# Twenty-three modulation vectors summed on VectorE instead of multiplied on TensorE

## The chip, the cores and the metric

The kernel runs on one core of one Trainium2 chip. The metric is the device time of one execution in microseconds (us), the median over several runs. Engines: PE is TensorE (PEld its weight load), DVE is VectorE, ACT is ScalarE, POOL is GpSimd, SP is SyncE. A name with q (SPq, POOLq) is an engine's own instruction queue, from which it also issues transfers.

## What is computed

Two blocks work on 256 tokens of width 1024. The first has two layers, each a gated feed-forward net, a mixer and a second gated net. Layer 0's mixer is a state-space scan (ssd) and also reads 256 context tokens, layer 1's is a pooling mixer. The second block has two layers of attention and an expert layer ("peer": 8 heads choose among 16384 experts). Every sub-layer takes a scale, a shift and a gate that depend on a conditioning vector `c`, not on the tokens:

```
m  = (silu(c)     @ ada_w[i] + ada_b[i]).reshape(-1, 9, 1024)      # first block, i = 0, 1
mc = (silu(c_ctx) @ ada_w[i] + ada_b[i]).reshape(9, 1024)          # the same for the context
x  = x + 0.5 * m[:, 2] * swiglu(modulate(x, g, m[:, 0], m[:, 1]), wg, wu, wd)
h  = h + 0.5 * mc[2] * swiglu(modulate(h, g, mc[0], mc[1]), wg, wu, wd)   # context, layer 0 only
mod = c_2_act @ w_ada + b_ada                                      # second block: 6 vectors a layer
```

That is 9 + 9 + 6 + 6 = 30 modulation vectors, each a product of one row of 1024 numbers with a 1024 x 1024 float32 matrix, 4 MB that is read once. The context needs a second result only for vectors 0 to 4 of layer 0, since nothing after the ssd mixer reads it.

## The kernel before

**Work on TensorE.** Activations stand as 8 tiles of 128 features by 256 tokens (512 with the context). Each weight unit, 128 x 1024 float32 (512 KB), is loaded by SP into one of four buffers (`raw`), and split in halves of 512 columns: ACT rounds a half to `whi` (L444), DVE subtracts to get `wlo` (L446). Three matmuls (`mm3`: low x high, high x low, high x high) then give float32 precision. `pump` keeps the splits three halves ahead of TensorE (`LS` = 3). The order in time: the first feed-forward net f0 (512 columns), the ssd mixer, f1 (256), f2, the pooling mixer, f3, attention 0, expert layer 0, attention 1, expert layer 1. Within a net, `ffn_up` takes 22 blocks of two units each (gate and up; psum tile `gu`), and after a block DVE and ACT make the product (`ft`, `sg`, `gh`, `gl`); `ffn_down` takes 8 blocks of three units (`dn`).

**The modulation vectors.** A vector is eight steps, one for each 128 rows of its matrix. A step (`ada_mm`) is four matmuls at four groups of 32 columns of the array: 32 columns of `sc` (silu of the conditioning vectors, three of them used) against 256 columns of the row tile each, summed in psum over the eight steps. In the profile it is eight PE instructions on the tile `ada`. After the eighth, ACT copies the result (`adarow`, L568), TensorE transposes it twice (`adat`, L575) and DVE adds the bias (`mods`, L581). Two vectors are made at the start (`adah`, `adar`), since nothing can begin without them.

**Where the other 28 stand.** In f0, f1 and f2 the planner `mix` puts row tiles among the weight units as units of their own, two at a time, and four at the end of a net (`KEEP`), where TensorE waits for a norm. SP loads them in that order, through the same queue. In the ssd mixer and the attentions the order on every engine is made by `Flow`, a list scheduler with a cost for each operation. There `ada_load` and `ada_work` are chains beside the others: 52 steps go into the ssd stage and 44 into the two attentions, in groups of two (ssd) or one (attention).

**Other names.** `btab` is a table of attention biases, written by POOL to DRAM in f0 (L1633); `csts` holds constants, `xt` the inputs; `rel` and `bk` feed the bias table. `Gen.need` makes sure that a vector is ready before its first reader.

Of the kernel before, what the change touches and what calls it, by code (L numbers as in the profile page):

```python
# [31 lines left out]
ATT_ADA = (3, 3)  # L32
# [11 lines left out]
SSD_ADA = 7  # L44
# [182 lines left out]

class Flow:
# [4 lines left out]
    TABLE_US, DMA_US, ADA_US, FAST, SOON, MORE = 1.28, 1.46, 3.5, 0, 2, 1  # L233

    def __init__(self, gen, slots, ada, raws, lat, early=0, group=1):
        slots = {**slots, "W": [f"W{n}" for n in range(gen.LS + 1)], **{k: [x for x in raws if x[0] == k] for k in "QR"}}
# [12 lines left out]
        self.adas, self.raws = {}, raws  # L249
        self.spawn(self.ada_load(ada, early), 0)  # L250
        self.spawn(self.ada_work(ada, group), 9)
# [108 lines left out]
    def ada_load(self, keys, early):  # L360
        for n, key in enumerate(keys):
            r = self.adas[key] = yield "take", "Q" if n < early else "R"
            yield "S", self.ADA_US if n >= self.FAST else self.DMA_US
            self.gen.nc.sync.dma_start(self.raws[r], self.gen.ada_src(*key))
            self.loading(("ada",) + key)

    def ada_work(self, keys, group):
        g = self.gen
        for n in range(0, len(keys), group):
            part = keys[n:n + group]  # L370
            yield "wait", *[("ada",) + k for k in part]
            yield "P", 0.43 * len(part)
            for key in part:
                g.ada_mm(key[3], self.raws[self.adas[key]])
                self.give(self.adas[key])
                self.set(("used",) + key)
            if key[3] == KT - 1:
                yield "A", 0.26
                self.spawn(self.ada_fin(key[:3], g.ada_row()), 1)

    def ada_fin(self, key, row):
        t = yield "take", "T"
        self.gen.ada_tag = t
        g = self.gen.ada_fin(*key, row)
        yield "P", 0.23
        next(g)
        yield "V", 0.1
        next(g, None)
        self.give(t)
        self.set(("mod",) + key)  # L390


class Gen:
    def __init__(self, tc, I, out):
        self.tc, self.nc, self.I, self.out = tc, tc.nc, I, out
        self.units = []
        self.subs = []
        self.cur = self.nd = self.ns = self.csub = 0
        self.raw, self.hl = {}, {}
        self.later = deque()  # L400
        self.sides = []
        self.ln_loaded = False
        self.ada_tag, self.no_split = "B", True
        self.loaded = set()
        self.ada_pool, self.took = None, {"w": deque(maxlen=self.LD), "ada": deque(maxlen=self.LA)}
        self.uid = 0
        self.sq_bufs = 2
# [3 lines left out]
    SSD_GROUP, ATT_GROUP, SSD_LAT, ATT_LAT = 2, 1, 0.06, 0.04  # L411
    LD, LD2, LA, LS, SUB, NW, SSD_Q = 4, 8, 4, 3, 512, 12, 8

    def add(self, tag, ap, n, kind="w"):
        u = len(self.units)
        self.units.append((tag, ap, n, kind))
        if kind == "w":
            for c in range(0, n, self.SUB):
                self.subs.append((u, c, min(self.SUB, n - c)))

    def room(self, i):

        if self.ada_pool is None:
            return i < self.cur + self.LD
        k = self.units[i][3]
        last = self.took[k]
        return len(last) < last.maxlen or last[0] not in self.raw

    def pump(self):
        while self.nd < min(len(self.units), self.cur + self.LD + self.LA) and self.room(self.nd):  # L430
            self.load(self.nd, self.p_raw)
# [20 lines left out]
    def load(self, i, pool):  # L452
        if self.units[i][0][0] == "gu" and len(self.units[i][0]) == 6 and self.units[i][0][5] == 0:
            t = self.p_first.tile([128, 512], F32, tag="first", name=f"raw{i}", bufs=2 * self.FIRST)
        else:
            kind = self.units[i][3] if self.ada_pool is not None else "w"
            if kind == "ada":
                t = self.ada_pool.tile([128, 1024], F32, tag="araw", name=f"raw{i}", bufs=self.LA)
            else:
                t = pool.tile([128, 1024], F32, tag="raw", name=f"raw{i}")  # L460
            self.took[kind].append(i)
# [5 lines left out]
    def _next(self):  # L467
        i = self.cur
        self.cur += 1
        self.pump()  # L470
        self.run_later()
        return i
# [20 lines left out]
    def get(self, tag, width=128):  # L493

        while self.units[self.cur][3] == "ada":
            self.ada_step()
# [35 lines left out]
    def ada_unit(self, which, l, m, k):  # L532
        self.add((which, l, m, k), self.ada_src(which, l, m, k), 1024, "ada")

# [3 lines left out]

    def ada(self, n):
        for _ in range(n):  # L540
            if self.cur < len(self.units) and self.units[self.cur][3] == "ada":
                self.ada_step()

    def ada_step(self):
        nc = self.nc
        i = self.cur
        self.cur += 1
        which, l, m, k = self.units[i][0]
        self.ada_mm(k, self.raw.pop(i))
        if k == KT - 1:  # L550
            row = self.ada_row()
            self.mod_sent.add((which, l, m))
            self.defer(4, lambda: [None for _ in self.ada_fin(which, l, m, row)])
        self.pump()
        self.run_later()
# [9 lines left out]
    def ada_row(self):  # L565
        self.uid += 1
        row = self.p_ada.tile([128, 256], F32, tag="adarow", name=f"adarow{self.uid}")
        self.nc.scalar.copy(row, self.ada_ps)  # L568
        return row

    def ada_fin(self, which, l, m, row):
# [5 lines left out]
        ns = 2 if which == 0 and l == 0 else 1  # L577
# [7 lines left out]
    def need(self, *keys):  # L585
        if not all(k in self.mod_ready for k in keys):
            left = {k for k in keys if k not in self.mod_ready and k not in self.mod_sent}
            while left and self.units[self.cur][3] == "ada":
                self.ada_step()
                left -= self.mod_sent  # L590
# [94 lines left out]
    def open_fed(self):  # L685
# [9 lines left out]
        self.ada_pool = self.p_ada  # L695
# [93 lines left out]
    def ffn_up(self, l, j, N, gh, gl, x, post, pw, first=0):  # L789

        for f in range(first, FT):
            ps = []
# [11 lines left out]
    def ffn_down(self, l, j, N, gh, gl, xs, gate_m, fed):  # L804
# [7 lines left out]
        self.ln_table()  # L812
        for d in range(KT):
            p = self.ps.tile([128, 512], F32, tag="C", name=f"dn{l}{j}{d}")
# [5 lines left out]
            for s, x in enumerate(xs):  # L820
                nc.vector.scalar_tensor_tensor(x[:, d], p[:, 256 * s:256 * s + 256], hg[s][:, d:d + 1],
                                               x[:, d], op0=ALU.mult, op1=ALU.add)
            if fed:
# [5 lines left out]
    FIRST = 3  # L829

    def ffn0(self, xs):
# [6 lines left out]
        with ExitStack() as es:  # L838
            es.enter_context(self.sqpool("f00"))
            pu = es.enter_context(self.pool("ffu"))  # L840
# [126 lines left out]
            gh = pg.tile([128, FT, N], F32R, name="gh")  # L967
            gl = pg.tile([128, FT, N], F32R, name="gl")
            self.ada_pool = pg
            bt = self.bias_table(pw)  # L970
# [13 lines left out]
            self.ffn_up(0, 0, N, gh, gl, lambda k: (uh[:, k], ul[:, k]), lambda: post, pw, self.FIRST)  # L984
            self.ffn_down(0, 0, N, gh, gl, xs, 2, None)
            self.ada_pool = None
# [39 lines left out]
    def ssd(self, XL, XC, px, u, fed):  # L1026
# [9 lines left out]
        with ExitStack() as es:  # L1036
# [10 lines left out]

            raws = {f"Q{n}": T1(f"sraw{n}", [128, 1024]) for n in range(2)}
            for n, (k, s) in enumerate((("m0", [4, 128]), ("m1", [4, 128]), ("hin", [4, 2, 64]), ("yo", [4, 2, 64]))):
                x = raws[f"Q{n // 2}"][:, n % 2 * 512:n % 2 * 512 + 512]  # L1050
                B[k] = x.rearrange("p (a b) -> p a b", a=4) if n < 2 else x.rearrange("p (a b c) -> p a b c", a=4, b=2)
                slots[k] = [k]
            raws.update({f"R{n}": XC[:, 4 * n:4 * n + 4].rearrange("p a b -> p (a b)") for n in range(2)})
            fl = Flow(self, {**slots, **{k: self.banks[k] for k in "ABCT"}}, self.ssd_ada, raws, self.SSD_LAT, self.SSD_Q,
                      self.SSD_GROUP)
# [31 lines left out]
            def rs_work():  # L1087
# [8 lines left out]
                for n in range(2):  # L1096
                    yield "wait", *[("u", k, x) for k in range(4 * n, 4 * n + 4) for x in range(2)]
                    fl.give(f"R{n}")
                fl.give("gr.0")
                fl.give("sq.0")  # L1100

            def early_work():
                yield "wait", *[("used",) + k for k in self.ssd_ada[self.SSD_Q - 2:self.SSD_Q]]
                for k in ("m0", "m1", "hin", "yo"):
                    fl.give(k)
# [409 lines left out]
            for k in ("T", "gr", "R", "m0", "m1", "hin", "yo"):  # L1515
                fl.free[k] = []
            fl.spawn(early_work(), 0)
# [101 lines left out]
    def bias_table(self, pool):  # L1619
# [11 lines left out]
        sb = pool.tile([8, 384], F32, name="bts")  # L1631
# [4 lines left out]
    def attention(self, l, XL, fed):  # L1636
# [5 lines left out]
        with ExitStack() as es:  # L1642
            es.enter_context(self.sqpool(f"at{l}"))
            self.p_ada = es.enter_context(self.pool(f"adap2{l}", 2))
            p2 = es.enter_context(self.pool(f"rawp2{l}"))
# [4 lines left out]
            for j in range(4):  # L1650
                for kv in range(2):
# [30 lines left out]
            raws = {f"R{n}": p2.tile([128, 1024], F32, name=f"R{n}_{l}") for n in range(self.LD2)}  # L1682
            st = {}
            fl = Flow(self, {"A": self.banks["A"] + self.banks["C"], "B": self.banks["B"], "T": self.banks["T"],
                             "w": list(work), "v": list(wide)}, self.att_ada[l], raws, self.ATT_LAT, group=self.ATT_GROUP)
# [435 lines left out]
    def peer(self, l, XL, last, fed, px):  # L2121
# [5 lines left out]
        with ExitStack() as es:  # L2127
# [57 lines left out]
            for e in range(120):  # L2185
                if e + 1 == 64:
                    self.side_rest()
                    er.close()
                    tail = es.enter_context(self.pool(f"pet{l}")).tile([128, 2, 4, 256], F32R, name=f"tail{l}")
                if e + 1 < 120:  # L2190
# [5 lines left out]
                wq.pop(e)  # L2196
            self.p_sq = Slices(act[0])
# [301 lines left out]
    GROUP, KEEP, QUIET, EVERY, HOLD = 2, 4, 5, 2, 4  # L2499

    def mix(self, gen, ada=(), every=1, start=0, bounds=()):


        a = deque(x for w in ada for x in ([w] if len(w) == 4 else [w + (k,) for k in range(KT)]))
        gen = list(gen)
# [121 lines left out]
```

## Time and profile before

| | us |
|---|---|
| median of 3 runs (lowest, highest) | 3321.62 (3319.46, 3324.21) |
| the profiled execution's own time | 3323.24 |
| span of its instructions | 3321.5 |
| PE busy | 3286.7 (99%) |
| DVE busy | 2356.7 (71%) |
| ACT busy | 1690.9 (51%) |
| POOL busy | 21.6 (1%) |

The page gives busy time by engine for the one profiled execution. PE's busy time overstates its work, since matmuls are pipelined and their ends are modelled; what a group of matmuls costs is read from the starts of what stands before and behind it. The mean granted clock of TensorE is 0.998 of full speed. 622 MB are moved, 187 GB/s on the mean.

### The profile page before, as it was taken

To read this page: it belongs to the slowest core of one execution; us is meant where nothing else is said; L and a number is where in the kernel's file an instruction comes from. 1 tells how busy PE (TensorE), PEld (TensorE's weight loads), DVE (VectorE), ACT (ScalarE), POOL (GpSimd) and SP (SyncE) were. 2 spreads that over 40 slices of the span, in tenths; PEclk is the share of its full clock that TensorE was granted. 3 is DMA by queue.
4 is the path that set the end of the run, shared out by engine and by line. 5 is a ranking of instruction groups with operands and counts; after the bars stand their busy time and mean duration, and the time that the engine had idled before them with its cause. 6 is when DMAs were issued, how large, how long until landed. Compare 5 with 4: busy or idle time off the path is not lost.

```text
span 3321.5 us, 71394 instructions
## 1 busy us (share of the span) xinstructions
PE 3286.7 (99%) x28517; PEld 3063.8 (92%) x28532; DVE 2356.7 (71%) x5253; ACT 1690.9 (51%) x3408; POOL 21.6 (1%) x40
## 2 busy tenths in 40 slices
PE   7999999999999999999999999999999999999999
PEld 5777778889999989989999999999889999999999
DVE  4333378886656667677898779866778888788765
ACT  4222255555555555566554444455666554444454
POOL 0000000000000000000000000000000000000000
PEclk9999999999999999999999999999999999999999
DMA  7644444446777655675555444455665554444554
GB/s 249 182 178 173 176 150 162 143 156 227 253 240 249 231 195 187 183 271 185 177 184 168 165 164 162 161 178 185 227 230 169 179 185 161 164 163 162 172 185 159
DMA packets 177790, 621.97 MB, mean 187 GB/s; under 512 B 19949, under 2 KB 23021, under 8 KB 177072
## 3 DMA queue, kind: packets, MB, share of 16 engines
q1 hardware_dynamic: 174912, 609.07, 54.2%
q0 software_dynamic: 2544, 8.32, 1.0%
q8 instruction: 224, 3.67, 0.5%
q14 instruction: 110, 0.90, 0.1%
HBM read 614.69 MB, written 2.62 MB: 186 GB/s over the span
## 4 chain that ended last, share of the span: by engine, by line
PE 97%; DMA 1%; DVE 1%; ACT 1%; issue 0%; SPq 0%; ACTq 0%; DVEq 0%
PE s L522 22%; PE up L522 22%; PE gu L522 18%; PE dn L522 9%; PE xbc L522 4%; PE ada L522 3%; PE g L522 3%; PE q L522 3%; PE wc L522 3%; PE wo L522 3%; PE z L522 1%; PE yd L522 1%; PE st L522 1%; DMA raw<-ffn_gu 1%; PE sc L522 0%; PE yo L522 0%
## 5 line engine op out<-in xcount | busy, mean ns | idle before, releaser
L446 DVE TENSOR_TENSOR wlo<-raw,whi 128x512 fp32r<-128x512 f32 x1846 | 1254.2, 685 | 732.0 <-ACT whi L444 713.4
L444 ACT CAST whi<-raw 128x512 fp32r<-128x512 f32 x1846 | 1126.3, 615 | 1009.9 <-PE up L522 376.1
L522 PE MATMUL s<-U,whi 128*128 128x256 f32 x4096 | 734.0, 281 | 0.0
L522 PE MATMUL up<-U,whi 128*128 128x256 f32 x3936 | 705.1, 282 | 0.0
L522 PEld LDWEIGHTS s<-U,whi 128*128 128x128 f32 x4096 | 632.4, 189 | 0.0
L522 PEld LDWEIGHTS up<-U,whi 128*128 128x128 f32 x3936 | 606.2, 189 | 0.0
L522 PE MATMUL s<-U,wlo 128*128 128x256 f32 x2048 | 581.3, 284 | 0.0
L522 PE MATMUL up<-U,wlo 128*128 128x256 f32 x1968 | 556.2, 283 | 0.0
L522 PEld LDWEIGHTS s<-U,wlo 128*128 128x128 f32 x2048 | 386.9, 189 | 0.0
L522 PEld LDWEIGHTS up<-U,wlo 128*128 128x128 f32 x1968 | 371.9, 189 | 0.0
L522 PE MATMUL gu<-U,whi 128*128 128x258 f32 x1408 | 254.4, 282 | 2.5 <-DVE U L732 2.5
L522 PEld LDWEIGHTS gu<-U,whi 128*128 128x128 f32 x1408 | 218.7, 190 | 3.3 <-DVE U L732 3.1
L522 PE MATMUL dn<-gh,wlo 128*128 128x256 f32 (+1 forms) x704 | 220.2, 313 | 0.3 <-DVE wlo L446 0.3
L522 PE MATMUL dn<-gl,whi 128*128 128x256 f32 (+1 forms) x704 | 218.2, 310 | 0.0
L522 PE MATMUL dn<-gh,whi 128*128 128x256 f32 (+1 forms) x704 | 217.9, 309 | 0.0
L2139 ACT ACTIVATE act<-s 128x256 f32<-128x256 f32 x256 | 98.4, 384 | 208.3 <-PE s L522 208.3
L522 PE MATMUL gu<-U,wlo 128*128 128x258 f32 x704 | 202.0, 287 | 0.0
L522 PEld LDWEIGHTS dn<-gh,wlo 128*128 128x128 f32 x704 | 134.3, 191 | 13.9 <-issue 3.3
L522 PE MATMUL gu<-uh,wlo 128*128 128x512 f32 x352 | 140.5, 399 | 2.9 <-DVE wlo L446 1.7
L522 PEld LDWEIGHTS dn<-gh,whi 128*128 128x128 f32 x704 | 134.3, 191 | 7.2
L522 PEld LDWEIGHTS dn<-gl,whi 128*128 128x128 f32 x704 | 134.3, 191 | 6.5
L522 PE MATMUL gu<-ul,whi 128*128 128x512 f32 x352 | 139.0, 395 | 0.7 <-DVE ul L905 0.6
(423 smaller groups left out, 5095.5 us busy)
## 6 DMA issues: line engine op xcount, KB each, us to landing
raw<-pdown SPq DMA_DIRECT2D x256, 512.0 KB, 3.3
raw<-pup SPq DMA_DIRECT2D x240, 512.0 KB, 3.3
raw<-ffn_gu SPq DMA_DIRECT2D x170, 512.0 KB, 4.4
raw<-ada_w SPq DMA_DIRECT2D x76, 512.0 KB, 4.4
raw<-ffn_dn SPq DMA_DIRECT2D x64, 512.0 KB, 4.3
raw<-w_ada SPq DMA_DIRECT2D x52, 512.0 KB, 6.0
XC<-ada_w SPq DMA_DIRECT2D x44, 512.0 KB, 4.4
R<-w_ada SPq DMA_DIRECT2D x44, 512.0 KB, 6.0
```

Of the source, the lines that this page charges most:

```text
L444: nc.scalar.copy(hi[:, :n], r[:, c:c + n])
L446: nc.vector.tensor_tensor(out=lo[:, :n], in0=r[:, c:c + n], in1=hi[:, :n].bitcast(F32), op=ALU.subtract)
L522: self.nc.tensor.matmul(ps, a, b, start=start, stop=stop, skip_group_check=skip)
L2139: self.other_table().activation(act[e // 64][:, e % 64], p, AF.Gelu)
```

## The change

Of the 28 vectors, 23 are no longer multiplied step by step on TensorE. The vector's row tiles are scaled by silu(c), which is one number per partition, and summed over the eight steps: the first step on ACT (`activation` with Copy and a scale), seven on DVE (`scalar_tensor_tensor`, 128 x 1024). Then four matmuls with a matrix of ones add up the 128 partitions (`adas`), and the copy, the transposes and the bias follow as before. Five vectors are still multiplied as before: 2, 4 and 3 of layer 0 (both conditionings needed), in the second half of f0's up part, and two of the second block as the fillers at ends of nets.

`mix`, its counters and `Flow`'s chains for the vectors are gone. Where steps stand is set by a rate: with every weight unit that TensorE takes, `ada_tick` adds ADA_RATE to a sum and issues a step for each whole number. f0 makes 10 sums and the three whole vectors, f1 to f3 nine sums, expert layer 0 four; ssd, pooling and attention none (pooling keeps its four fillers). The row tiles are loaded by POOL's queue, not SP's, into 8 tiles (f0's two halves, expert layer), 6 (f1 to f3) and 3 or 4 for the whole vectors. Room for them in f0 comes from the product's tiles `gh` and `gl`, whose rows from 14 on (`Rows`, `MID` = 13) are taken only at the middle of the up part, and from moving f0's inputs to the right side of the memory.

```diff
+ADA_SUMS = {"up0": [(0, 0, m) for m in (5, 7, 6, 8)] + [(0, 1, 1), (0, 1, 0)],
+            "down0": [(0, 1, m) for m in (2, 4, 3, 5)],
+            "ffn": [(0, 1, m) for m in (7, 6, 8)] + [(1, 0, m) for m in (1, 0, 2, 4, 3, 5)],
+            "peer": [(1, 1, m) for m in (1, 0, 3, 5)]}
+ADA_WHOLE = {"mid0": [(0, 0, m) for m in (2, 4, 3)], "fill": [(1, 1, 2), (1, 1, 4)]}
+ADA_RATE = {"half0": 1.0, "up0": 2.1, "mid0": 1.4, "down0": 1.55, "up": 0.33, "down": 0.55, "peer": 0.65}
...
+    def ada_fill(self, n=99):
+        for x in "sw":
+            while self.abuf[x] and self.aload[x] and n:
+                key, b = self.aload[x].popleft(), self.abuf[x].popleft()
+                self.nc.gpsimd.dma_start(b, self.ada_src(*key))
+                self.got[key] = b
...
+    def ada_tick(self):
+        if self.rate is not None:
+            self.due += ADA_RATE[self.rate]
+            x = "w" if self.rate == "mid0" else "s"
+            while self.due >= 1.0:
+                self.due -= 1.0
+                if self.whole if x == "w" else self.sums:
+                    self.ada_step(x)
...
+    def ada_sum(self, which, l, m, k, r):
         nc = self.nc
+        s = self.sc[:, k, 2 * which:2 * which + 1]
+        acc = self.accs[0]
+        if k == 0:
+            nc.scalar.activation(acc, r, AF.Copy, scale=s)
+            return
+        nc.vector.scalar_tensor_tensor(acc, r, s, acc, op0=ALU.mult, op1=ALU.add)
         if k == KT - 1:
+            self.accs.rotate(-1)
             self.mod_sent.add((which, l, m))
+            def close():
+                ps = self.ps.tile([128, 256], F32, tag="T", name=f"adas{which}{l}{m}")
+                for c in range(4):
+                    self.mm(ps[32 * c:32 * c + 32, :], self.ones[:, :32], acc[:, c * 256:(c + 1) * 256], True, True, True)
+                self.ada_close(which, l, m, self.ada_row(ps), 3)
+            self.defer(3, close)
...
+            self.ada_open("half0", ADA_SUMS["up0"], [pr.tile([128, 1024], F32, name=f"uraw{n}") for n in range(8)], accs)
```

Three places show the moves. On POOL, from the program's start to the first transfers of f0 (`uraw` are the row tiles of f0's up part), its queue was:

```order
L2485 DMA csts_74<-cst 128x384
L1626 DMA rel_531<-rel 32x8
L1627 DMA bk_532<-bkt 33x384
L1633 DMA btab_530<-bts_828 1024x1x384
L1058 DMA tri_3405<-cst 128x256
```

and is now, with what each row waits for (DMASW are landings of POOL's own earlier transfers):

```order
L2545 DMA csts_74<-cst 128x384
L538 DMA uraw0_541<-ada_w 128x1024
L538 DMA uraw1_542<-ada_w 128x1024
L538 DMA uraw2_543<-ada_w 128x1024
L538 DMA uraw3_544<-ada_w 128x1024
L538 DMA uraw4_545<-ada_w 128x1024
L538 DMA uraw5_546<-ada_w 128x1024
L538 DMA uraw6_547<-ada_w 128x1024
L538 DMA uraw7_548<-ada_w 128x1024 [waits DMASW0_49]
L1682 DMA rel_558<-rel 32x8 [waits DMASW1_49,DVE_49]
L1683 DMA bk_559<-bkt 33x384 [waits DMASW2_49]
```

Eight row tiles stand ahead of `rel`, and the first seven wait for nothing.

On DVE, one block of f1's up part (four splits `wlo`, the two outputs `ft`, the product `sg` and its low part `gl`) was:

```order
L446 TENSOR_TENSOR wlo_8217<-raw_8051,whi_8216 128x512
L446 TENSOR_TENSOR wlo_8235<-raw_8086,whi_8234 128x512
L446 TENSOR_TENSOR wlo_8252<-raw_8086,whi_8251 128x512
L446 TENSOR_TENSOR wlo_8270<-raw_8137,whi_8269 128x512
L1002 COPY fb_8286<-gu_8215 128x1
L1003 TENSOR_TENSOR ft_8287<-gu_8215,ffr_7359 128x256
L1002 COPY fb_8286<-gu_8250 128x1
L1003 TENSOR_TENSOR ft_8288<-gu_8250,ffr_7359 128x256
L1006 SCALAR_TENSOR_TENSOR sg_8285<-ft_8288,fb_8286,sg_8285 128x256
L787 TENSOR_TENSOR gl_7319<-sg_8285,gh_7318 128x256
```

and is now:

```order
L428 TENSOR_TENSOR wlo_8604<-raw_8449,whi_8603 128x512
L428 TENSOR_TENSOR wlo_8622<-raw_8488,whi_8621 128x512
L579 SCALAR_TENSOR_TENSOR araw_7066<-araw_7063,sc,araw_7066 128x1024
L428 TENSOR_TENSOR wlo_8641<-raw_8488,whi_8640 128x512
L428 TENSOR_TENSOR wlo_8659<-raw_8537,whi_8658 128x512
L1071 COPY fb_8675<-gu_8602 128x1
L1072 TENSOR_TENSOR ft_8676<-gu_8602,ffr_7127 128x256
L1071 COPY fb_8675<-gu_8639 128x1
L1072 TENSOR_TENSOR ft_8677<-gu_8639,ffr_7127 128x256
L1075 SCALAR_TENSOR_TENSOR sg_8674<-ft_8677,fb_8675,sg_8674 128x256
L822 TENSOR_TENSOR gl_7091<-sg_8674,gh_7090 128x256
```

A sum step (L579) stands between two splits, in about six of ten blocks.

On PE, at the third turn of the ssd mixer (`xt` transposes that turn's inputs, `st` makes its states), there was:

```order
L522 MATMUL xbc_4430<-su_3361,whi_4285 128x512
L522 MATMUL ada_4314<-XC,sc 32x256 x8
L522 MATMUL xbc_4430<-su_3361,wlo_4286 128x512
L522 MATMUL xbc_4430<-su_3362,whi_4285 128x512
L522 MATMUL xbc_4430<-su_3361,whi_4285 128x512
L1309 MATMUL xt_4466<-csts,x_3383 128x128 x4
```

and there is:

```order
L499 MATMUL xbc_4382<-su_3417,wlo_4335 128x512
L499 MATMUL xbc_4382<-su_3418,whi_4334 128x512
L499 MATMUL xbc_4382<-su_3417,whi_4334 128x512
L1366 MATMUL xt_4442<-csts,x_3439 128x128 x4
L499 MATMUL xbc_4382<-su_3417,wlo_4335 128x512
```

The two steps (eight matmuls) are gone from between the blocks of the projection `xbc`.

## Rows read from the trace of the kernel before

**Rows 1.** The page's chain that ended last, by engine.

```profile
PE 97%; DMA 1%; DVE 1%; ACT 1%; issue 0%; SPq 0%; ACTq 0%; DVEq 0%
```

**Rows 2.** Stretches, tile ada alone: length, then busy (instructions) of PE, PEld, ACT.

```profile
50.00:436.00 386.00, 32.29 (x464) 11.48 (x464) 2.58 (x7) 1.00 0.51 175
456.00:790.00 334.00, 26.77 (x400) 10.43 (x400) 2.63 (x7) 1.00 0.48 162
790.00:1000.00 210.00, 16.44 (x252) 6.78 (x256) 1.11 (x3) 1.00 0.72 247
1000.00:1237.00 237.00, 17.40 (x268) 6.77 (x256) 1.83 (x5) 1.00 0.67 229
1427.00:1534.00 107.00, 12.88 (x164) 3.15 (x160) 1.14 (x3) 1.00 0.67 239
2367.00:2481.00 114.00, 15.34 (x192) 3.78 (x192) 1.12 (x3) 1.00 0.69 249
```

**Rows 3.** Chain of waits in order of time: start us, length us, what.

```profile
12.40 10.82 DMA adar<-ada_w
...
191.82 11.14 PE gu L522 x48
203.96 11.15 PE gu L522 x48
...
415.69 19.09 PE dn L522 x84
...
502.39 2.87 PE z L522 x24
...
1466.48 0.57 PE ada L522 x8
1467.05 3.11 PE wc L522 x24
...
1488.37 0.22 PE adat L575 x2
```

**Rows 4.** Stretches, all tiles: length, busy of PE, PEld, DVE, ACT, POOL; clock, DMA share, GB/s.

```profile
10.00:15.00 5.00, 1.08 (x16) 0.66 (x16) 3.38 (x5) 3.85 (x8) 0.00 (x0) 1.00 1.06 382
40.00:45.00 5.00, 5.00 (x50) 3.87 (x49) 4.13 (x10) 0.62 (x1) 0.00 (x0) 1.00 0.08 22
50.00:436.00 386.00, 384.25 (x1994) 294.38 (x1994) 132.62 (x230) 114.14 (x206) 3.25 (x5) 1.00 0.51 175
456.00:790.00 334.00, 332.83 (x2645) 280.74 (x2659) 270.44 (x585) 190.47 (x436) 0.00 (x0) 1.00 0.48 162
1237.00:1361.00 124.00, 124.00 (x1034) 123.91 (x1034) 91.69 (x214) 70.41 (x131) 0.00 (x0) 0.99 0.57 180
1427.00:1534.00 107.00, 106.38 (x873) 89.33 (x870) 78.53 (x202) 70.52 (x174) 6.63 (x12) 1.00 0.67 239
```

**Rows 5.** Start of the program on POOL: start us, length us, instruction.

```profile
1.26 0.68 POOL L2485 DMA_DIRECT2D csts<-cst  x1 [0.81 <-POOLq L2619]
```

**Rows 6.** Waits of PE, 456 to 790 us: us in total, times, longest us.

```profile
PE cb L522 <- ACT sraw L1341: 0.2, 1, 0.2
```

**Rows 7.** Groups, shapes apart: busy us, mean ns of one, idle before.

```profile
L1137 DVE SCALAR_TENSOR_TENSOR ca<-pad,cwh,ca 128x512 f32<-128x512 f32 x80 | 59.6, 746 | 0.7 <-ACT ca L1134 0.3
L1137 DVE SCALAR_TENSOR_TENSOR ca<-pad,cwh,ca 128x256 f32<-128x256 f32 x16 | 7.6, 480 | 0.2
```

**Rows 8.** Waits of DVE in f3's up part, 1237 to 1361 us.

```profile
DVE wlo L446 <- ACT whi L444: 16.2, 23, 1.6
DVE gl L787 <- ACT gh L786: 9.9, 21, 0.5
DVE sg L1006 <- ACT sg L1005: 4.2, 21, 0.5
```

**Rows 9.** Transfers: count, KB each, median us from issue to landing.

```profile
keys<-keys POOLq DMA_DIRECT2D x2, 1024.0 KB, 6.5
btab<-bts POOLq DMA_DIRECT2D x1, 1536.0 KB, 34.8
```

More of the change, by code (lines that the diff above doesn't have):

```diff
@@ L225, in tile, with __init__, more, __getitem__ @@
         return self.t[:, ring[-1], :shape[1]]
+class Rows:
+    def __init__(self, t):
+        self.t, self.n, self.rest = t, t.shape[1], None
+    def more(self, t):
+        self.rest = t
+    def __getitem__(self, i):
+        return self.t[:, i[1]] if i[1] < self.n else self.rest[:, i[1] - self.n]
 class Flow:
-    TABLE_US, DMA_US, ADA_US, FAST, SOON, MORE = 1.28, 1.46, 3.5, 0, 2, 1
-    def __init__(self, gen, slots, ada, raws, lat, early=0, group=1):
-        slots = {**slots, "W": [f"W{n}" for n in range(gen.LS + 1)], **{k: [x for x in raws if x[0] == k] for k in "QR"}}
+    TABLE_US, DMA_US, SOON, MORE = 1.28, 1.46, 2, 1
+    def __init__(self, gen, slots, lat):
+        slots = {**slots, "W": [f"W{n}" for n in range(gen.LS + 1)]}
         self.gen, self.clock, self.LAT = gen, {}, lat
@@ L358, in unit @@
                 self.give(w)
[L360 to L390, printed above, removed]
 class Gen:
@@ L455, in load @@
         else:
[L456 to L461, printed above, removed]
+            t = pool.tile([128, 1024], F32, tag="raw", name=f"raw{i}")
+            self.took.append(i)
         self.nc.sync.dma_start(t[:, :self.units[i][2]], self.units[i][1])
@@ L537, in ada_src, with steps, ada_open @@
         return src[l, k * 128:(k + 1) * 128, m * 1024:(m + 1) * 1024]
+    def steps(self, vectors):
+        return [v + (k,) for v in vectors for k in range(KT)]
+    def ada_open(self, rate, sums=(), bufs=(), accs=(), whole=(), wbufs=()):
+        self.abuf = {"s": deque(bufs), "w": deque(wbufs)}
+        self.accs, self.rate, self.due = deque(accs), rate, 0.0
+        self.sums.extend(self.steps(sums))
+        self.whole.extend(whole)
+        self.aload = {"s": deque(self.sums), "w": deque(self.whole)}
+        self.ada_fill()
@@ new lines, in ada_shut @@
+    def ada_shut(self):
+        self.rate = None
+        while self.sums:
+            self.ada_step("s")
+        while self.whole:
+            self.ada_step("w")
+        self.flush()
+    def ada_fill(self, n=99):
[12 more added lines that the diff above has]
+                    self.ada_step(x)
@@ L539, in ada, with ada_step @@
     def ada(self, n):
         for _ in range(n):
-            if self.cur < len(self.units) and self.units[self.cur][3] == "ada":
-                self.ada_step()
-    def ada_step(self):
-        nc = self.nc
[L546 to L549, printed above, removed]
+            if self.whole and self.whole[0] in self.got:
+                self.ada_step("w")
+    def ada_step(self, x):
+        which, l, m, k = key = (self.sums if x == "s" else self.whole).popleft()
+        b = self.got.pop(key)
+        if x == "s":
+            self.ada_sum(which, l, m, k, b)
+        else:
+            self.ada_mm(k, b)
+            if k == KT - 1:
+                self.ada_close(which, l, m, self.ada_row(self.ada_ps))
+        self.abuf[x].append(b)
+        self.ada_fill()
@@ L576, in ada_fin @@
         yield
-        ns = 2 if which == 0 and l == 0 else 1
+        ns = 2 if which == 0 and l == 0 and m < 5 else 1
         bias = self.colv(f"ada_b{l}" if which == 0 else f"b_ada{l}", m * 8, 8).rearrange("p (c h) -> p h c", h=2)
@@ L586, in need @@
         if not all(k in self.mod_ready for k in keys):
[L587 to L590, printed above, removed]
+            while self.sums and any(k not in self.mod_sent | self.mod_ready for k in keys):
+                self.ada_step("s")
             self.flush()
@@ L694, in open_fed @@
         self.open_ada()
-        self.ada_pool = self.p_ada
+        self.by_use = True
+        tiles = [self.p_ada.tile([128, 1024], F32, name=f"araw{n}", bufs=1) for n in range(12)]
+        self.ada_open(None, ADA_SUMS["ffn"], tiles[:6], tiles[6:8],
+                      self.steps(ADA_WHOLE["fill"])[self.KEEP:], tiles[8:])
     def zero_last(self, us):
@@ L791, in ffn_up @@
         for f in range(first, FT):
+            if f == (first if N == 512 else 2):
+                self.rate = "up0" if N == 512 else "up"
+            if N == 512 and f == self.MID:
+                self.half()
             ps = []
@@ L812, in ffn_down @@
         self.ln_table()
+        if N == 256:
+            self.rate = "down"
         for d in range(KT):
+            if d == KT - 1:
+                self.rate = None
+                while N == 512 and self.sums:
+                    self.ada_step("s")
             p = self.ps.tile([128, 512], F32, tag="C", name=f"dn{l}{j}{d}")
@@ L984, in ffn0 @@
             self.ffn_up(0, 0, N, gh, gl, lambda k: (uh[:, k], ul[:, k]), lambda: post, pw, self.FIRST)
+            self.ada_shut()
+            eu.close()
+            pr = eu.enter_context(self.pool("ffd", side="right"))
+            self.ada_open("down0", ADA_SUMS["down0"], [pr.tile([128, 1024], F32, name=f"draw{n}") for n in range(8)], accs,
+                          self.steps(ADA_WHOLE["fill"])[:self.KEEP], self.mid_bufs)
             self.ffn_down(0, 0, N, gh, gl, xs, 2, None)
-            self.ada_pool = None
+            self.ada_shut()
+            self.by_use = False
     def ffn(self, l, j, XL, gate_m, fed):
@@ L1095, in rs_work @@
                 fl.set(("rs", 1))
-                for n in range(2):
-                    yield "wait", *[("u", k, x) for k in range(4 * n, 4 * n + 4) for x in range(2)]
-                    fl.give(f"R{n}")
+                yield "wait", *[("u", k, x) for k in range(KT) for x in range(2)]
                 fl.give("gr.0")
                 fl.give("sq.0")
[L1102 to L1105, printed above, removed]
             def u_work(k, n):
@@ L1630, in bias_table @@
         self.mm(ps, rel, bk, True, True)
-        sb = pool.tile([8, 384], F32, name="bts")
+        sb = bk[:8]
         nc.scalar.copy(sb, ps)
@@ L2497, in setup @@
             self.mods[1, l] = cp.tile([128, 6, 1, 8], F32, name=f"mods1{l}")
[L2499 to L2505, printed above, removed]
-        bounds = [b for b in bounds if b < len(gen)] + [len(gen)]
-        for n, f in enumerate(gen):
-            f()
-            left = [b for b in bounds if b > n]
-            count = 0
-            if n + 1 in bounds:
-                count = min(self.KEEP, KT - a[0][3]) if a else 0
-            elif n >= start and (n + 1) % (every * self.GROUP) == 0:
-                count = min(self.GROUP, len(a) - self.KEEP * len(left))
-                if left[0] - n - 1 <= self.QUIET * every and a and a[0][3] <= self.HOLD:
-                    count = 0
-            for _ in range(min(count, len(a))):
-                self.ada_unit(*a.popleft())
-        while a:
-            self.ada_unit(*a.popleft())
```

135 lines of the change are left out of this document (55 added, 80 removed).

## The prediction

> **What bounds the kernel now.** I read four views. First the page's chain that ended last: PE holds 97% of it, every other engine 1% or less [rows 1]. So a matmul taken from PE shortens the program, unless something else is close behind. Second, the stretches on tile `ada` alone, for where the 224 steps stand: eight PE instructions are a step, so 58 steps lie in f0, 50 in the ssd mixer, 32 in f1, 32 in f2 with the pooling mixer, 20 and 24 in the attentions, 4 each at the ends of f0 and f3 [rows 2]. Third the chain in order of time, for what a step costs: `ada`'s own busy time misleads, since matmuls overlap. Between two groups of 48 `gu` a pair of steps stands: the starts are 12.14 us apart, 48 matmuls at 19.09/84 = 0.227 us make 10.91, so a pair costs 1.24 us. A single step between like groups shows 0.57 and makes the next 24 matmuls 3.11 long instead of 2.87, so 0.8 us. A vector's transposes take 0.22 [rows 3]. Fourth the same stretches with all tiles, for what is second: in the ssd mixer DVE is busy 270 of 334 us, in f3's up part 91.7 of 124, in the first attention 78.5 of 107 [rows 4]. Still PE waits for DVE or ACT almost nowhere: the ssd stage has one such wait of 0.2 us [rows 6]. So its `ada` steps are not fillers of idle PE time; they displace other matmuls.
>
> **The change, part by part.** A sum costs PE only its close: four matmuls of a step's shape (0.8) and the transposes (0.22), about 1.0 us for a vector that took eight steps, 5 to 6 us. 23 closes replace 184 steps.
>
> *Ssd mixer.* 25 pairs at 1.24 and seven pairs of transposes go: 32.5 us. DVE is at 270 of 334; with 27 us less it stands at 88%, so the order should still follow PE. I take 85% of it, −27.6.
>
> *Attentions.* 20 and 24 single steps at 0.8 with three transposes each: 16.7 and 19.9 us. DVE in the first rises to 78.5 of 92, 85%. I take 90%: −15 and −17.9.
>
> *f0.* Before: 29 pairs at 1.24, and for each of six pairs that a vector's transposes split, these (0.22) and two singles in the pair's place (1.60 − 1.24): 39.4. After: ten closes at 0.8 and 13 transposes at 0.22, 10.9; of the three vectors kept I read from the new order 12 single steps (9.6) and six pairs (7.4); and about 1 us where, at the middle, a close and its transposes follow each other directly. Together 28.9, so −10.5.
>
> *f1, f2.* f1 loses 14 pairs and three transposes (18) and keeps a group of four at its end; it gets three closes: −15. f2 loses 12 pairs, with transposes 15.8, and gets three closes: −12.6. Two steps each way at the pooling mixer's start: −1.
>
> *The new sums on DVE.* No row has this operation at 128 x 1024. Its form takes 480 ns at 256 columns and 746 at 512 [rows 7]; going on in line, 746 + 2 × 266 = 1278 ns. In the up part of f1 to f3 (0.33 a unit, two units a block, seven of eight on DVE) that is 0.58 × 1.28 = 0.74 us a block. A block lasts 124/22 = 5.64 us; DVE is busy 4.17 of it, waits 14.1/22 = 0.64 inside the product, and 16.2/22 = 0.74 for `whi` [rows 8]. Only the last is free, and it is just filled. Then the stock of three halves, which covered DVE during the product, no longer refills between products. Bounds for a net: below nothing is excluded, since DVE gets no work less; 0 if the order lets the sums slip between, 12 × 1.28 = 15 if each of its 12 sums comes out of PE's time. Nearest row is the free 0.74 against 0.74 needed, so I take +3 for each net. f3 has no steps to lose but four fillers that stay, and gets three closes: +6 in all. In f0 DVE has room: 133 of 386 us [rows 4], and 4.2 × 7/8 × 1.28 = 4.7 us of sums in a block of 11 makes 77%.
>
> *Expert layer 0.* Four closes: +4. DVE's 28 sums lie beside PE there (+1 for this and the odd stall).
>
> *The start.* POOL's first transfer was issued at 1.26 us and took 0.68 [rows 5]. Now eight row tiles follow it, seven waiting for nothing, so all are in flight within some 8 us. There the machine waits for data, not for PE: the chain holds `adar`, a transfer from 12.40 to 23.22 [rows 3], and from 10 to 15 us the transfer engines are full at 382 GB/s, while at 40 they rest at 22 [rows 4]. Eight tiles are 4.19 MB, at 382 GB/s 11.0 us. They are needed only from f0's third block on. I take +10, between 0 (they are served last) and 11. The Trainium skill, "DMA: Bandwidth & Descriptors", section "Issuing engines are not separate DMA queues", says that transfers begun by different engines end up on the same 16 transfer engines and interleave there; by that rule the new queue gives no lane of its own, and the start pays near the upper bound. The 382 GB/s beside a waiting chain agrees.
>
> **The sum,** against the profiled execution's 3323.24 us: start +10, f0 −10.5, ssd −27.6, f1 −15 + 3, f2 −12.6 + 3, pooling −1, f3 +6, attentions −15 and −17.9, expert layer +5: −72.6, so 3250.6. The median of the runs lies 1.6 below that execution, which gives 3249; I say 3250.
>
> **The rivals.** *DVE takes the place of PE in the nets.* For it: 0.74 free, 0.74 needed, no reserve. Against it: `pump` keeps three halves of stock, and the down parts let DVE catch up. If all 12 sums of each up part come out of PE's time: 3 × (15.4 − 3) = +37, 3287; with a little in the mixers 3290.
>
> *The mixers give nothing.* If what follows in the ssd mixer and attentions is late by as much as the steps took, 27.6 + 32.9 come back: 3310. For it DVE's 81% in the ssd stage; against it the single PE wait of 0.2 us [rows 6].
>
> *Everything comes off, and the start is hidden.* Without the +10, the 9 for DVE and the discounts in the mixers (4.9 and 3.7): 3222.
>
> *POOL's queue is too slow: slower than before.* In f0 up to the middle a tile is taken every 11.1/4.2 = 2.7 us, in its down part every 3.3. Those of the two parts that the first eight don't cover are 40 and 24. DVE works in order: a sum whose tile is late stands before the next `wlo`, and PE has three halves (8 us, one product's length apart) in hand. The 40 have about 141 us and the stock of 8 twice, the 24 have 102 and the same: 64 tiles at an interval i lose about 64 i − 275 us once both parts are late, which eats the gain of 73 from i = 5.4 us on. At 6.5 us it would be +141, some 3390. Rows on both sides: POOL's `keys`, 1 MB, landed 6.5 us after issue, 3.25 for 512 KB even without overlap, its 1.5 MB write `btab` took 34.8, 11.6 for 512 KB [rows 9]. The first is a read of long rows like the row tiles, so I lean on it. The Trainium skill, "SBUF — State Buffer", section "SBUF: two separate sides", warns that a transfer issued by GpSimd can be held up while VectorE runs certain fast copies, since its descriptors can't be written then; by that rule, with DVE now busier, this rival would come true. No row here shows it for a stream.
>
> **How the numbers follow.** Forecast .60, DVE in the nets .16, no gain in the mixers .07, everything off .08, POOL too slow .09. The range 3215 to 3300 holds the forecast, the first rival and the third; the second and the slow one stay outside (.16). What a measurement of this kernel tells from no change is about 0.2%, 6.6 us, so between 3315 and 3328 counts as the same: of the cases only edges of the second and the last rival fall there, .02. Faster .90, slower .08.
>
> **What would show it.** Start: the first `gu` some 10 us later, with the eight row tiles landing before 35 us. Mixers: the ssd stage near 306 us, the attentions near 92 and 97, PE still without waits; were the stages as long as before, with PE waiting for DVE, the second rival holds. Nets: PE waiting for `wlo` in f1 to f3's up parts, about 3 us a net (15 is the first rival), and the new DVE group at 1.28 us. Closes: 23 groups `adas` at 0.8. POOL: row tiles landing within 21 us (8 × 2.7) of issue in f0; DVE waiting there for transfers would prove the last rival. The forecast is wrong above all if DVE, off the chain now, turns out to end waits in the nets and mixers both.

## The result and the profile after

The changed kernel takes 3282.4 us (3282.1 to 3286.0, four runs) against 3322.0 (3319.5 to 3324.2): the ratio is 0.9884, interval 0.9866 to 0.9901. It is faster by 39.6 us or 1.2%; 72.6 us were forecast, and the time lies inside the forecast's range. The profiled execution took 3286.0, the slowest of the four; its span is 3284.2 against 3321.5, so the stages below add up to some 37 us and not to 39.6.

The stages, each measured in both traces from the first product of a name to the first of the next (us):

| stage | before | after | change | forecast |
|---|---|---|---|---|
| start, to the first `gu` | 25.8 | 37.4 | +11.6 | +10 |
| f0 up, down | 276.3, 141.4 | 292.3, 137.9 | +12.5 | −10.5 |
| ssd mixer | 346.2 | 316.6 | −29.7 | −27.6 |
| f1 | 210.7 | 198.4 | −12.3 | −12 |
| f2 | 210.9 | 199.9 | −11.0 | −9.6 |
| pooling, f3 | 215.8 | 229.4 | +13.6 | +5 |
| attention 0, 1 | 107.2, 110.7 | 96.9, 95.5 | −10.3, −15.2 | −15, −17.9 |
| expert layer 0, second part (`up`) | 390.9 | 395.1 | +4.1 | +5 |

What the table leaves out changed by less than 1 us. In the ssd mixer, f1 and f2 the forecast holds to about 2 us. The shortfall of 36 stands in f0 (23), the pooling mixer with f3 (9) and the attentions (7); the other stages give 3 back. Four places of the trace after show what happened.

**The start.** The timeline's rows on POOL and ACT (start, length, instruction, idle before and what ended it):

```profile
1.26 0.69 POOL L2545 DMA_DIRECT2D csts<-cst  x1 [0.81 <-POOLq L2630]
1.94 3.66 POOL L538 DMA_DIRECT2D uraw<-ada_w  x7
...
16.97 2.19 ACT L931 ACTIVATE sq<-XL 128x512 f32<-128x512 f32 x4 [11.55 <-DMA XL<-xt]
```

Stretches of the same trace (columns as in [rows 4]):

```profile
20.00:25.00 5.00, 0.04 (x4) 0.07 (x7) 0.76 (x2) 1.50 (x3) 0.00 (x0) 1.00 1.05 385
40.00:45.00 5.00, 5.00 (x20) 3.88 (x18) 3.59 (x7) 1.99 (x4) 0.00 (x0) 0.85 1.05 387
```

The first input `XL` lands at 17 us; before, the same ACT instruction began at 9.09. The transfer engines are as full as before (385 GB/s), and at 40 us, where they had rested at 22 GB/s [rows 4], they still are.

**f0's up part.** Stretches around one stall:

```profile
125.00:130.00 5.00, 5.00 (x23) 3.99 (x23) 0.00 (x0) 0.00 (x0) 0.00 (x0) 1.00 0.73 172
130.00:135.00 5.00, 3.07 (x15) 2.28 (x14) 1.77 (x3) 2.25 (x4) 0.00 (x0) 1.00 0.50 80
135.00:140.00 5.00, 1.96 (x9) 1.25 (x7) 0.21 (x1) 0.63 (x2) 0.22 (x1) 1.00 0.48 137
140.00:145.00 5.00, 0.00 (x0) 0.00 (x0) 2.11 (x2) 0.00 (x0) 0.84 (x2) 0.55 0.77 269
145.00:150.00 5.00, 3.89 (x9) 3.12 (x10) 4.96 (x8) 2.67 (x4) 2.01 (x4) 0.50 0.93 324
150.00:155.00 5.00, 5.00 (x26) 3.44 (x26) 3.46 (x5) 1.50 (x4) 0.17 (x2) 0.93 1.03 416
```

Waits of DVE, 95 to 150 us (total, times, longest):

```profile
DVE wlo L428 <- ACT whi L426: 11.1, 3, 9.4
DVE acc L579 <- DMA uraw<-ada_w: 7.7, 2, 6.6
```

PE stands still twice, between starts 2.2 and 9.6 us apart, and DVE with it: first a weight is late (`whi` waits for its unit), then a sum's row tile is, and the next `wlo` stands behind the sum. From 130 to 140 us the transfer engines move only 80 to 137 GB/s. `btab` is under way there: issued at 103.4, landed after 35.9 us. The row tiles issued behind it in POOL's queue took 29 to 36 us to land, the weights issued meanwhile in SP's queue 21 to 28. Behind the stall the granted clock is 0.50, the lower level of 1.2 GHz, until about 150 us.

**Every product of f0's up part.** A stretch of 24 us, tile `gu` alone (busy of PE, PEld, DVE, ACT; clock, DMA share, GB/s), before, and then after:

```profile
53.00:77.00 24.00, 24.00 (x107) 19.86 (x107) 2.06 (x3) 2.38 (x4) 1.00 0.54 200
```

```profile
62.00:86.00 24.00, 24.00 (x104) 18.79 (x103) 2.07 (x3) 1.79 (x3) 1.00 0.74 257
```

Over all 1056 products the median distance of two starts is 0.227 us before and 0.234 after, at the full clock in both: 7.4 us in sum. In f0's down part those that read `gh` stay at 0.227, those that read `gh2` (the tile with the rows from 14 on) come every 0.234.

**Pooling and the attention.** PE's wait for `box`, an input of the pooling mixer, 1112 to 1230 us:

```profile
PE pbox L499 <- DMA box<-box: 4.9, 1, 4.9
```

Before, PE had no such wait. The ssd mixer (first row) and attention 0 (the other three), to be held against [rows 4]:

```profile
467.00:784.00 317.00, 315.74 (x2285) 278.73 (x2285) 276.96 (x601) 194.06 (x442) 0.00 (x0) 0.99 0.30 91
1412.00:1472.00 60.00, 59.94 (x447) 54.57 (x447) 48.98 (x135) 45.19 (x121) 7.64 (x13) 1.00 0.48 141
1472.00:1485.00 13.00, 10.24 (x76) 9.08 (x75) 10.93 (x27) 8.01 (x17) 0.53 (x1) 0.88 0.70 237
1485.00:1509.00 24.00, 24.00 (x190) 23.73 (x189) 17.48 (x38) 15.05 (x33) 0.00 (x0) 0.92 0.45 133
```

The ssd mixer stays full with DVE at 277 of 317. The attention's end does not: PE misses 2.8 of 13 us, and the clock falls to 0.88 and 0.92, where before no stretch of it was below 1.00.

### The profile page after: what moved, and what is told of

Same layout as the page of the kernel before. It is cut to its first block, busy times and chain, and to the rows that moved or that the text cites. A ratio compares the mean times of both kernels' runs of the same rounds, so it can differ in the third digit from the quotient of the medians.

```text
span 3284.2 us, 69149 instructions
## 1 busy us (share of the span) xinstructions
PE 3215.1 (98%) x27244; PEld 3039.4 (93%) x27244; DVE 2528.5 (77%) x5410; ACT 1706.6 (52%) x3431; POOL 139.9 (4%) x264
## 4 chain that ended last, share of the span: by engine, by line
PE 56%; DVE 1%; ACT 0%; issue 0%; ACTq 0%
PE s L499 22%; PE up L499 22%; PE g L499 3%; PE q L499 3%; PE wc L499 2%; PE wo L499 1%; PE sc L499 0%; PE l L499 0%; DVE wlo L428 0%; PE pv L499 0%; PE pt L1903 0%; PE css L499 0%; ACT whi L426 0%; PE qss L499 0%; PE yss L499 0%
## 5 line engine op out<-in xcount | busy, mean ns | idle before, releaser
L499 PE MATMUL gu<-uh,wlo 128*128 128x512 f32 x352 | 144.1, 409 | 12.5 <-DVE wlo L428 9.2
```

Of the source, the lines that this page charges most:

```text
L499: self.nc.tensor.matmul(ps, a, b, start=start, stop=stop, skip_group_check=skip)
```

## The experiments

Theory: what is missing was lost to transfers that met (start, `btab`, `box`) and to the slower spacing in f0. Rival: the new sums on DVE took it. Each edit is on the changed kernel, 3282.4 us, unless said. The runs were made in three sets; the kernel before, measured beside each, took 3322.5, 3322.8 and 3323.6, so differences between sets below 2 us mean little.

**e1_gate.** A copy of one column on POOL, ahead of the eight loads, waits for a weight unit:

```diff
+            nc.gpsimd.tensor_copy(out=ur[0][:, :1], in_=self.raw[min(self.raw)][:, :1])
             self.ada_open("half0", ADA_SUMS["up0"], ur, accs)
```

> The eight row tiles of f0 wait for one weight unit that lands some 10 us after the first product starts. Theory (transfers in the way): the start chain is as before, first gu near 26 us instead of 37.4, and the time falls by about 11 us, to 3271. Rival (the bytes only move): the tiles then collide with the next weights, PE waits for them between 40 and 70 us, and less than half of it is gained, 3277 or more. Theory DVE (what is missing lies in the new sums): the start is not its subject, the later stall of about 9 us for wlo near 136 us stays.

Measured 3271.9, −10.5. The first `gu` is at 25.1, f0's up part takes 291.3 as before the edit (292.3), and the wait for `wlo` is still there (8.9). The start's cost is these transfers, and held back they don't collide later.

**e2_btab_late.**

```diff
-                if f == 4:
+                if f == 15:
                     next(bt)
```

> btab is written at the 16th block of f0 instead of the 5th, where the stream of row tiles is half as dense. Theory (transfers in the way): the stall of 2.2 and 9.6 us near 131 and 137 us and the lowered clock behind it vanish, about 14 us, to 3268; up to 2 us come back at the new place, as in the kernel before. Rival (the stream alone is too dense for its queue; 2.7 us a tile): the stall stays at its place or moves by a few blocks, time within 3 us of 3282. Theory DVE: no change.

Measured 3296.6, +14: a miss, for both sides. The old stall is gone, and a worse one stands at the new place. PE's wait, 30 to 480 us, and a stretch in it:

```profile
PE ada L499 <- DMA mraw<-ada_w: 24.3, 1, 24.3
```

```profile
260.00:265.00 5.00, 0.00 (x0) 0.00 (x0) 0.00 (x0) 0.00 (x0) 0.00 (x0) 0.50 0.50 82
```

There only three tiles stand ahead of PE. The one issued behind `btab` in POOL's queue, at 238.7, took 35.5 us and landed just behind it; a weight issued later in SP's queue, at 240.5, landed earlier, after 22.4. PE waited for no weight there. So the density of the stream was not the point; how long the stock of loaded tiles lasts behind the write was.

**e3_box_first.** f2's last fillers don't refill their tiles; the pooling mixer does it behind `box`:

```diff
-        self.ada_fill()
+        if not self.hold:
+            self.ada_fill()
...
             nc.gpsimd.dma_start(box..., self.I["box"])
+            self.hold = False
+            self.ada_fill()
```

> The four refills behind f2's last fillers are issued after box, not ahead of it. Theory (order in POOL's queue): PE's wait of 4.9 us for box falls to about 0 to 1, the pooling stage loses 4 to 5 us, to 3278. Rival (the wait only changes its name, since weights and norm end it too): under 1.5 us gained.

Measured 3275.8, −6.6; the pooling mixer falls from 25.2 to 19.1 us, and of the wait there is left

```profile
PE pbox L500 <- DMA box<-box: 1.1, 1, 1.1
```

**e4_three.** The three edits together.

> The three edits together. If they are independent costs of transfers: 11 + 14 + 4.5 less, about 3253, near the forecast of 3250. If the row tiles collide elsewhere when they are held back: 3262 or more.

Measured 3279.0. The sum of the three as measured (−10.5 + 14.2 − 6.6) gives 3279.5: within the noise they are independent, and the forecast missed by the second alone.

**e5_align.** Two pads of 32 bytes. By the program's allocation `uh` starts at byte 68800 of a partition before (64 × 1075) and at 186336 after (64 × 2911 + 32); `gh2`, `gl2` lie at an odd multiple of 32 too.

```diff
+            pu.tile([128, 8], F32, name="upad")
...
-        rel = pool.tile([33, 8], F32, name="rel")
+        rel = pool.tile([33, 16], F32, name="rel")[:, :8]
```

> uh and ul moved down by 32 bytes, and gh2 and gl2 up by 32, so that all four start at a multiple of 64 bytes, as in the kernel before; nothing else changes. Theory (place in memory): the 1056 products of f0's up part come every 0.227 us again instead of 0.234, 7.4 us, and the 192 of the down part that read gh2 and gl2 too, 1.3 us: 8.7 less than 3282, 3274. Rival (the matmuls are slower because DVE, POOL's transfers and PE work at once, as they never did before): 0.234 stays, and the time.

Measured 3275.7, −6.7, with f0's up part 6.6 shorter; the median distance is 0.227 again, and in the stretch shown above stand

```profile
62.00:86.00 24.00, 24.00 (x106) 19.56 (x105) 2.05 (x3) 1.78 (x3) 1.00 0.76 255
```

DVE, POOL and the transfers run beside it as before the edit, so the rival falls. The down part gained 0.6, half of what was expected: the products that read `gh2` come every 0.229 to 0.231 now, not 0.227. So a start at a multiple of 64 bytes is not all that a place does.

**e6_btab_ssd.** The product for `btab` at the end of f0, the write behind the ssd mixer's first two loads; its tiles move to a pool of their own.

```diff
-                if f == 4:
-                    next(bt)
...
             nc.gpsimd.dma_start(B["z.0"], self.I["cst"][:, 768:1024])
+            next(self.bt)
```

> btab is written at the start of the ssd mixer, when POOL's queue has nothing else and the transfers move 90 GB/s; gh2 and gl2 come to start at a multiple of 64 bytes by it. Theory (a write of 35 us and a dense stream in one place): no stall in f0's up part, 11.5 us and some 3 us of lowered clock behind it, and 1.3 for gh2: 3266. Rival (any 35 us of this write hold up what is beside it): a new wait of over 5 us in the ssd mixer, 3272 or more.

Measured 3263.7, −18.7. f0's up part takes 15.2 less; where the stall was, one row:

```profile
140.00:145.00 5.00, 5.00 (x23) 4.00 (x22) 3.27 (x4) 1.75 (x3) 1.06 (x2) 1.00 0.82 281
```

The write still takes 33.4 us, and a weight issued beside it in SP's queue 20.8, but the ssd mixer 315.6 against 316.6: it holds nobody up where the stock lasts. Not all of the 18.7 is the write's: f1's and f2's down parts are 1.4 and 1.3 shorter, and the products of f0's down part that read `gh` come every 0.229 instead of 0.227. The new pool moved `gh` and its like by 1600 bytes, from one multiple of 64 to another; that this did it was not tested apart.

**e7_double_sums.**

```diff
-ADA_RATE = {..., "up": 0.33, ...}
+ADA_RATE = {..., "up": 0.66, ...}
```

> In f1 to f3's up parts two sums are issued where one was (ADA_RATE 0.66 for 0.33), so that all of a net's sums fall there; the work of the whole program is the same. Theory of the forecast (DVE has 0.74 us a block free, the sums then need 1.48): each of some 20 blocks lacks 0.74, PE waits for wlo, +15 us a net, 3320 or more. Rival (DVE's waits inside the product can be filled too, and PE has stock): within 3 us of 3282.

Measured 3297.1, +14.7, between the two. The nine vectors were used up by the end of f2, so only two nets had the double rate: f1's up part took 8.0 more, f2's 11.0, f3's nothing. PE's waits in f1's:

```profile
PE gu L499 <- DVE wlo L428: 4.2, 4, 1.1
```

15 a net were expected from 0.74 us a block missing; 8 and 11 came, with some closes that moved from the down part among them. f3's up part, left without any sum, takes 133.6 against 133.9 with twelve. So at the first rate the sums of an up part cost next to nothing, and at twice the rate they do cost: the free time of DVE that [rows 8] gave is a bound that lies between the two.

**e8_four.** The edits of e1, e3, e5 and e6.

> Four edits together: row tiles of f0 held back until a weight unit has landed, box ahead of the refills, btab in the ssd mixer, and the four tiles at multiples of 64 bytes. If each is a cost of its own: 10.5 + 6.6 + 14.5 + 8.7 less 1.3 that two share, 38.5 below 3282.4, some 3244. If they hide one another: 3255 or more.

Measured 3240.0 (3239.2 to 3244.2), ratio to the kernel before 0.9755, interval 0.9739 to 0.9771: faster than the kernel before and the changed one. The parts alone sum to −42.5; −42.4 came. f0 takes 410.0 against 417.7 before the change. The page:

```profile
PE 3193.0 (99%) x27229; PEld 3026.1 (93%) x27244; DVE 2528.8 (78%) x5410; ACT 1706.0 (53%) x3431; POOL 140.0 (4%) x265
```

**e9_sp_queue.**

```diff
-                self.nc.gpsimd.dma_start(b, self.ada_src(*key))
+                self.nc.sync.dma_start(b, self.ada_src(*key))
```

> The row tiles are loaded by SP's queue instead of POOL's, in the order in which the program asks for them, so eight of them stand in f0 behind the first halves of the weights. Theory (the start cost is their place ahead of what the start needs): first gu near 28 us instead of 37.4, some 9 less. Against it: a weight unit now stands in SP's queue behind sum tiles whose buffers DVE has not freed, which can cost PE waits in f0's up part; by the one alone 3273, if the second holds 3285 or more. If neither matters, 3282.

Measured 3283.2. The first `gu` is at 25.9 (−11.5) and the pooling mixer 5.6 shorter, but f1's up part takes 9.3 more and expert layer 0's second part 4.4, so the gains are used up. The theory of the start came true; the cost of the shared queue came too, in f1 and not in f0. In f1, SP waited with a row tile at the head of its queue:

```profile
SPq L538 <- DVE araw L579: 32.9, 11, 4.7
```

f0's up part takes 292.1 here, as in the changed kernel, although no row tile stands behind `btab` in POOL's queue any more. The stall is still there, PE's longest wait and the stretch:

```profile
PE gu L499 <- DVE sg L1040: 9.8, 1, 9.8
120.00:130.00 10.00, 1.09 (x6) 0.65 (x4) 0.48 (x1) 1.11 (x2) 0.00 (x0) 0.68 0.78 212
```

`btab` took 35.6 us, and a weight issued in SP's queue meanwhile, at 101.0, 27.7. So a stall of this length comes also where nothing stands behind the write in its queue, though here weights and row tiles share the other one.

**e10_half_start.** The copy of e1 into the fifth tile instead of the first.

> Four of the eight first row tiles wait for the weight unit, the other four go at the program's start as before: half the dose of the first experiment. Theory (bytes ahead of a full start): 2.1 MB at 382 GB/s, 5.5 us of the 11 stay; 3277. Rival (what delays the start is one blocked transfer or the queue, not the bytes): all or nothing, 3271 or 3282.

Measured 3274.1, the first `gu` at 26.0. It tells nothing of the dose: the copy still stands ahead of all eight loads in POOL's order, so all eight waited, as in e1. Whether four tiles would cost half stays open.

**e11_btab_act_queue.**

```diff
-        nc.gpsimd.dma_start(self.btab, ...)
+        nc.scalar.dma_start(self.btab, ...)
```

> btab is written at its old place, the 5th block of f0, but by ACT's queue, so that no row tile stands behind it in POOL's. Theory (the transfer engines are shared): weights and row tiles come late all the same, the stall of about 11 us near 131 to 146 us stays within 4 us, 3279 to 3283. Rival (order in POOL's queue): the stall vanishes, 3268.

Measured 3269.3, −13.1: the time of the rival. PE waits 0.9 us for `wlo` where it waited 9.2, DVE 2.4 for row tiles where it waited 7.7. Transfers issued from 95 to 145 us, first of the changed kernel, then of this one:

```profile
uraw<-ada_w POOLq DMA_DIRECT2D x12, 512.0 KB, 29.7
raw<-ffn_gu SPq DMA_DIRECT2D x6, 512.0 KB, 21.2
```

```profile
uraw<-ada_w POOLq DMA_DIRECT2D x15, 512.0 KB, 20.0
raw<-ffn_gu SPq DMA_DIRECT2D x7, 512.0 KB, 14.9
```

Row tiles and weights are still late, but eight tiles at one per 2.7 us last 21 us, and 20.0 is under it where 29.7 is not. That the order in POOL's queue did it is not shown, for the edit also changed the write itself. In ACT's queue, in the same stretch, it went as

```profile
q10 hardware_dynamic: 1032, 1.57, 21.3%
```

that is 1024 packets of 1536 bytes, each 0.23 us of a transfer engine on the median; in POOL's queue the trace has 336 packets of 4608 bytes, each 0.73 us. The first and the last packet lie 37 us apart here, so the write was not over sooner, but it kept the 16 engines busy for 10.6 us instead of 14.6. Weights in SP's queue, which never stood behind it, landed sooner too.

**e12_small_sums.** On e8:

```diff
-        nc.vector.scalar_tensor_tensor(acc, r, s, acc, ...)
+        nc.vector.scalar_tensor_tensor(acc[:, :64], r[:, :64], s, acc[:, :64], ...)
```

> The fourth kernel of the last set, with the sums of DVE cut to 64 of 1024 columns (the vectors of these steps are not computed): all transfers, closes and waits stay, DVE loses some 161 x 1.2 us. Theory (the sums lie beside PE): within 4 us of 3240. Forecast's term (they cost 3 us in each of three nets): 3231. If DVE sets the pace anywhere else: below 3225.

Measured 3236.8 (3233.8 to 3239.8), 3.2 under e8 (3239.2 to 3244.2): the theory, and near the noise, since the two ranges touch. 161 sums take 0.28 us instead of 1.28, which frees 161 us of DVE's time and shortens the program by about 3. By the two traces it is in the nets: f1, f2 and f3 are 2.1, 0.8 and 3.6 shorter, of which other stages of these single executions give 1.6 back. The rival that the sums on DVE took what is missing falls.

## Why the forecast came out as it did

**What held.** PE was the bound, and `ada`'s steps displaced other products: the ssd mixer gave 29.7 where 27.6 were forecast. The start cost 11.6 (forecast 10, just over its bound of 11), and e1 shows that the eight transfers did it. The estimate for the sum was 1278 ns; the profile has

```profile
L579 DVE SCALAR_TENSOR_TENSOR acc<-uraw,sc,acc x42: 1274/1280/1287, 65.6 to 206.5; 128x1024 f32<-128x1024 f32 x42
```

The closes came as priced, 0.77 and 0.22. The rivals "DVE takes the place of PE" and "the mixers give nothing" didn't come. That 3282 lies near the 3287 of the first of them, and inside the range, is chance. The term of +3 a net for DVE, 9 in all, was too high: e12 puts it at about 3 by the medians, 6.5 by the nets alone.

**What failed: f0, by 23 us.** The step said −10.5, from counts and prices of `ada` steps alone, with "in f0 DVE has room". That is right as far as it goes: with the other things taken away (e8) f0 gives −7.7. It put two others at nothing, which together make 20 to 22 of the 23.

- The diff moved f0's inputs to another place in memory, and I priced only its instructions. The place cost 7 us: e5 gave 6.6 back in the up part and 0.6 in the down part.
- `btab` met the new stream. The last rival had the mechanism, a late row tile that stands before the next `wlo`, but worked it out from a mean interval (from 5.4 us on). POOL's tiles kept up in the mean; what broke was one write of 35.9 us, against a stock of tiles that lasts 21. It cost 13 (e11) to 15 us (e6): the standstill of some 11 and, behind it, products at the lower clock, which came every 0.43 us instead of 0.23 for about 4 us. The row was there [rows 9], and I used it only as a price for 512 KB. Which side of the write does it stays in part open. Behind it, in the same queue, a tile lands only when it has landed (e2). But beside it, in SP's queue, weights take 21 to 28 us as well, and in e9, with nothing behind the write, the stall is as long as it was. Already before the change ACT waited 11.7 us there for a weight, and PE lost 1.7.

**Pooling and f3, by 9.** The pooling mixer alone is 7.3 longer, where −1 was forecast. I counted fillers and closes, not that the fillers' tiles are refilled, 2 MB at once, in the queue in which `box` comes next, and that each refill waits there until PE has read its tile. By e3 that is 6.6. The order of POOL's queue had shown it.

**The attentions, by 7.** I took 90% of the removed steps; 62% and 76% came. The rows show PE idle for 2.8 us at the end of the stage and a lowered clock behind it. I read it so that without the steps the chain through the softmax is nearer to PE, but no run tested this, and the cause stays open.

The weighed rule on shared transfer engines, from the Trainium skill, "DMA: Bandwidth & Descriptors", section "Issuing engines are not separate DMA queues", agrees at the start (385 GB/s, +11.6). It is not all: with `btab` moved to ACT's queue the same bytes at the same time cost 13 us less (e11). The rival weighed with the Trainium skill, "SBUF — State Buffer", section "SBUF: two separate sides", did not come, and the stream from POOL's queue ran beside a busy DVE. That section speaks of certain fast copies; whether the new sums count among them no run here shows. In 100 us of f1's up part of the changed kernel, with DVE at 82.6, PE missed 0.3:

```profile
800.00:900.00 100.00, 99.72 (x825) 98.74 (x825) 82.64 (x181) 55.84 (x106) 5.81 (x11) 1.00 0.74 255
```

## What to carry to other kernels

When a change adds a stream of transfers, list what else is issued while it runs, in the same queue first, and compare the longest of it with what the stock lasts, in us, not with the mean rate. A move of a tile in memory is an edit with a price of its own: compare the distance of like products before and after. Price a start by bytes: what is needed late should wait for something that lands late.

## What was not expected of the hardware

Products of 512 float32 columns that read `uh` and `ul` came every 0.227 us where these start at a multiple of 64 bytes and every 0.234 where they start 32 bytes beside one; 32 bytes of padding took it back (e5). No other offset was tried, and the multiple of 64 is not a rule for every tile here: `gh2` came down only to 0.229 to 0.231 by it, and `gh` rose from 0.227 to 0.229 between two such places (e6). A transfer issued behind a write of 1.5 MB in one queue landed after 35.5 us (e2), though the engines then moved only 82 GB/s. And the same write, issued by ACT instead of POOL, went in other packets and left the transfers beside it faster (e11).
